# Loading the second quarter of w by row set instead of by quadrant, in a matmul with a decayed running sum

## The chip, the cores and the metric

One core of one Trainium2 chip runs the whole problem. The metric is the device time of one launch in microseconds (us). The engines are named as in the profile: PE (TensorE), with PEld for its weight loads, DVE (VectorE), ACT (ScalarE), POOL (GpSimd) and SP (SyncE). PE, DVE, ACT and POOL compute; SP, ACT and POOL also issue transfers (DMAs), which 16 DMA engines carry out.

## The reference

```python
B, S, D = 16, 2048, 1024          # x: (B, S, D), w: (D, D), decay: (D,), all float32
xw = x @ w
out[:, 0, :] = xw[:, 0, :]
for t in range(1, S):
    out[:, t, :] = decay * out[:, t - 1, :] + xw[:, t, :]
```

## The kernel before, in words

The kernel works on x in 64 chunks of 512 time steps, two chunks to a group. POOL loads a chunk as bfloat16 (`load`, L105), DVE transposes it in 32 by 32 blocks (`turn`, L115), ACT or DVE regroups it into the tile `xt` (`part`, L123), and PE multiplies it with w (`matmul`, L131). For each of the eight blocks n of 128 output columns PE sums eight contraction blocks k into PSUM. DVE then scans along time with the decays, ACT and POOL help with half of the positions, DVE transposes back and SP stores. The work of each engine is written out by hand: a dictionary `agenda` (L520) names, for each step, a string of deeds that is performed in that order, and every instruction is pinned to its place.

The change lies in the first deeds, `agenda[-99]` (L521), which begin

```python
-99: "M0 M1 U0 M2 M3 U1 U2 w0 W1 w2 W3 K0 K1 K2 K3 E0 E1 G0 ... G7 q4 w5 Q4 W6 W7 D E8 ..."
```

`M` is `load_half`: half a chunk of x in four transfers of 128 KB, one per quadrant (32 partitions). M0 and M1 are the halves of chunk 0, M2 and M3 those of chunk 1. `U` is `load_part`: one quarter of w. All of these are issued by POOL, in this order, on one queue. The program gives POOL's transfers eight semaphores in turn, so each of them waits, before it is issued, until the POOL transfer eight places ahead has landed: U0 waits for M0, M2 for M1, M3 for U0, U1 for M2, U2 for M3.

w is stored as bfloat16 in `wsb`. A quarter (h, e) of it is the column half h (512 columns) of the rows of parity e. The quarter (0, 0) is loaded by SP and ACT at the very start; U0, U1 and U2 are the quarters (0, 1), (1, 0) and (1, 1). In the staging tile, partition 32q + p holds, for m = 0 to 3, the row 256q + 64m + 2p + e of w. The 128 rows of one m, 32 out of each of the four 256-row bands q, are called a row set here. They are exactly the contraction block k = 2m + e, and are copied into `wsb` by one deed per m (`settle`, L326): `W` on DVE, `w` on ACT. For U0 the deeds are `q4` and `Q4` (the row set m = 0, split at L375 into the columns of n = 0 and the rest), `w5`, `W6` and `W7` (m = 1, 2, 3). For U1 they are W8 to W11 on DVE, for U2 they are w12 to w15 on ACT.

PE begins with dummy matmuls (`spin`, L344). Then, for n = 0 to 3, it takes the even k of chunk 0 (both halves, L633), then the odd k of chunk 0 (L636), which are the ones that need U0, then all k of the first half of chunk 1 (L640, which needs the deeds E8 to E11, the transposes of M2), then the second half (L644, which needs E12 to E15, the transposes of M3). After these it goes on to n = 4 and above, even k first (which need W8 to W11), then odd k (which need w12 to w15).

The functions that the diff touches, with the line numbers of the profile:

Of the kernel before, what the change touches and what calls it, by code (L numbers as in the profile page):

```python
# [14 lines left out]
def _ap(ap_obj: bass.AP, new_ap, extra_offset=0):  # L15
    return dataclasses.replace(
        ap_obj,
        ap=[list(p) for p in new_ap],
        offset=ap_obj.offset + extra_offset,
    )  # L20
# [5 lines left out]
def kernel(  # L26
# [26 lines left out]
    nc = tc.nc  # L53
    pin = tc.keep_in_program_order
    B, S, D = x.shape
    assert w.shape == (D, D)

    NQ = 4
    P = 32
    CQ = D // NQ  # L60
    K = CQ // P
    M = K // 2
# [4 lines left out]
    CH = D // 2  # L67
# [12 lines left out]
    def quad(q):  # L80
        return slice(q * P, (q + 1) * P)
# [59 lines left out]
    class Tile:  # L141
# [39 lines left out]
        def copy(self):  # L181
            self.xs = sb.tile([128, 2 * TL], FP32, name=f"xs{self.lot % 3}")[:, 0:self.T]
            parts = self.ps if isinstance(self.ps, tuple) else (self.ps,)
            size = self.T // len(parts)
            for i, ps in enumerate(parts):
                pin(nc.scalar.copy(out=self.xs[:, i * size:(i + 1) * size], in_=ps))  # L186
# [99 lines left out]
    class Outlet:  # L286
# [8 lines left out]
        def store(self, b, t0):  # L295
# [4 lines left out]
            for j in range(0, self.nj, nj):  # L300
# [11 lines left out]
    stage = {(0, 0): room[0][:, 0:size],  # L312
             (0, 1): room[0][:, size:size * 3 // 2].bitcast(BF16),
             (1, 0): room[1][:, 0:size // 2].bitcast(BF16),
             (1, 1): room[1][:, size // 2:size].bitcast(BF16)}

    def load_w(queues, h, e):
        for i, q in enumerate((0, 2, 1, 3)):
            pin(queues[i % len(queues)].dma_start(  # L319
                out=stage[h, e][quad(q)].rearrange("p (m d) -> p m d", m=M),  # L320
                in_=_ap(w, [[2 * D, P], [2 * P * D, M], [1, CH]],
                        (q * CQ + e) * D + h * CH)))

    def settle(h, e, m, copy):
        src = stage[h, e][:, m * CH:(m + 1) * CH]
        pin(copy(out=wcols[:, 2 * m + e, h],  # L326
                 in_=src.rearrange("p (q r i) -> p q r i", q=NQ, r=R)))
# [21 lines left out]
    for q in range(NQ):  # L349
        pin(nc.sync.dma_start(  # L350
            out=rows[q * P:q * P + R],
            in_=_ap(decay, [[P, R], [CH, 2], [1, P]], q * CR)))
# [8 lines left out]
        spin(3 if q < NQ - 1 else 2, gates[q])  # L361

    def load_part(i):
        load_w((nc.gpsimd,), *((0, 1), (1, 0), (1, 1))[i])

    def part_one(i, copy):
        part(i // 8, copy, i % 4, i % 4 + 1, *halves[i // 4 % 2])
# [1 line left out]
    def settle_one(i, copy):  # L369
        settle(i // 8, i // 4 % 2, i % 4, copy)  # L370
# [102 lines left out]
    def turn_and_load(c):  # L473
# [16 lines left out]
        "w": lambda i: settle_one(i, nc.scalar.copy),  # L490
        "M": load_half,
        "U": load_part,
        "E": lambda i: turn(i // 8, *halves[i // 4 % 2], i % 4, i % 4 + 1),
        "F": lambda i: part_one(i, nc.vector.tensor_copy),
# [229 lines left out]
```

## Time and profile before

| | |
|---|---|
| median of 3 runs | 903.8 us (903.74 to 904.62) |
| the profiled execution | 903.77 us, span 902.0 us |
| granted TensorE clock | 1.0 |
| PE busy | 892.4 us (99%) |
| DVE, ACT, POOL busy | 824.9 (91%), 687.6 (76%), 656.6 (73%) us |
| POOL's transfers of w (L319, U0 to U2) | 12 of 128 KB, median 5.1 us from issue to landing |
| POOL's half-chunk transfers of x (M0 to M3) | 16 of 128 KB, median 5.9 us |

The span runs from the first to the last instruction that the profiler saw. Idle time of an engine other than the one that sets the end costs nothing by itself. In the lines of the time view, the first column is the start in us from the span's start, the second the duration, and the bracket at the end tells how long the engine had been idle before, and what ended that.

### The profile page before, as it was taken

Reading aid. Unit: us, or ns where it says so; the run is one execution under the profiler, and the core shown is the slowest. Engines: PE = TensorE matmul, PEld = TensorE weight load, DVE = VectorE, ACT = ScalarE, POOL = GpSimd, SP = SyncE. Lnnn points to the kernel's source line nnn. Section 1 sums busy time; section 2 is a strip of 40 time slices with the busy share of each in tenths; the row PEclk is TensorE's granted clock in tenths of the full one; section 3 lists DMA queues with packets and bytes.
Section 4 is the critical chain, followed back from the end, with each engine's and each line's share of the span. In section 5 each row is a group of like instructions: output and inputs, shape, how many; then the busy total and the mean of one; then the engine's idle time right before and its main releaser. Section 6 shows DMA issues by size and latency. Waiting matters only on the chain.

```text
span 902.0 us, 12224 instructions
## 1 busy us (share of the span) xinstructions
PE 892.4 (99%) x4127; PEld 412.1 (46%) x4209; DVE 824.9 (91%) x635; ACT 687.6 (76%) x962; POOL 656.6 (73%) x755
## 2 busy tenths in 40 slices
PE   9999999999999999999999999999999999999998
PEld 5544444444444444444444444444444444444444
DVE  4999998999999999999998999999999999999998
ACT  4889967777877877878778778777787787787743
POOL 7888678777767778777677686777777777776532
PEclk9999999999999999999999999999999999999999
DMA  9999999999999999999999999999999999999858
GB/s 191 194 215 220 229 243 218 215 218 249 244 243 254 231 258 251 251 243 250 225 234 227 223 234 224 232 228 226 233 230 227 227 231 225 226 228 222 176 146 239
DMA packets 403182, 204.77 MB, mean 227 GB/s; under 512 B 9392, under 2 KB 402096, under 8 KB 403120
## 3 DMA queue, kind: packets, MB, share of 16 engines
q1 hardware_dynamic: 265808, 134.77, 60.6%
q0 software_dynamic: 137024, 68.70, 56.9%
q8 instruction: 33, 0.54, 0.2%
q10 hardware_dynamic: 288, 0.52, 0.2%
q14 instruction: 29, 0.24, 0.1%
HBM read 138.42 MB, written 134.22 MB: 302 GB/s over the span
## 4 chain that ended last, share of the span: by engine, by line
PE 97%; DMA 1%; issue 1%; POOL 0%; DVE 0%; ACT 0%; DVEq 0%; POOLq 0%
PE ps L131 96%; PE spare L131 1%; DMA xb<-in_x_dram 1%; DMA ot<-in_w_dram 1%; POOL ot L319 0%; DVE so L233 0%; POOL xb L105 0%; PE ps L415 0%; PE spare L415 0%; ACT xb L422 0%; DVE wsb L375 0%; DVEq L375 0%; POOLq L708 0%
## 5 line engine op out<-in xcount | busy, mean ns | idle before, releaser
L131 PE MATMUL ps<-xt,wsb 128*128 128x512 bf16 x3934 | 860.8, 378 | 4.5 <-DVE wsb L375 0.2
L131 PEld LDWEIGHTS <-wsb 128*128 128x128 bf16 x4160 | 406.7, 98 | 478.7 <-ACT wsb L326 0.8
L208 POOL TENSOR_TENSOR xs<-h,xs 128x512 f32<-128x512 f32 (+1 forms) x190 | 242.8, 1278 | 188.2 <-ACT h L169 85.0
L186 ACT COPY xs<-ps 128x1024 f32<-128x1024 f32 (+1 forms) x190 | 188.8, 994 | 153.6 <-PE ps L131 143.2
L278 DVE STREAM_TRANSPOSE ot<-so 128x1024 f32<-128x1024 f32 (+2 forms) x264 | 300.2, 1175 | 2.3 <-POOL so L202 1.1
L266 POOL TENSOR_TENSOR so<-h,xs 128x512 f32<-128x512 f32 (+1 forms) x190 | 241.1, 1271 | 42.6 <-ACT h L169 27.1
L123 ACT COPY xt<-xw 128x2048 bf16<-128x2048 bf16 (+1 forms) x136 | 242.3, 1790 | 7.8 <-DVE xw L115 7.8
L105 POOL DMA_DIRECT2D xb<-in_x_dram x264 | 173.9, 660 | 3.4 <-DMA ot<-in_w_dram 1.3
L169 ACT ACTIVATE h<-so,dec 128x512 f32<-128x512 f32 (+1 forms) x190 | 145.5, 766 | 27.8 <-DVE so L213 24.5
L115 DVE STREAM_TRANSPOSE xw<-xb 128x2048 f32<-128x2048 f32 (+1 forms) x78 | 147.3, 1901 | 6.7 <-DMA xb<-in_x_dram 6.7
L213 DVE TENSOR_TENSOR_SCAN so<-spare,keep,xs 128x512 f32<-128x512 f32 (+1 forms) x97 | 119.9, 1239 | 26.7 <-POOL xs L208 26.3
L213 DVE TENSOR_TENSOR_SCAN so<-spare,xs 128x512 f32<-128x512 f32 x93 | 113.3, 1220 | 27.2 <-POOL xs L208 24.4
L169 ACT ACTIVATE h<-ps,dec 128x512 f32<-128x512 f32 (+1 forms) x189 | 129.5, 685 | 0.0
L233 DVE TENSOR_TENSOR_SCAN so<-dec,ps 128x1024 f32<-128x1024 f32 x34 | 76.9, 2260 | 0.8 <-ACT h L169 0.6
L233 DVE TENSOR_TENSOR_SCAN so<-dec,keep,ps 128x1024 f32<-128x1024 f32 (+2 forms) x35 | 74.7, 2137 | 0.0
L270 ACT COPY keep<-so 128x1 f32<-128x1 f32 x136 | 25.2, 188 | 9.2 <-DVE so L233 8.7
L204 ACT COPY so<-keep 128x1 f32<-128x1 f32 x97 | 18.4, 191 | 2.5 <-DVE ot L278 2.3
L131 PE MATMUL spare<-xt,wsb 128*128 128x512 bf16 (+1 forms) x64 | 12.9, 332 | 0.0
L131 PE MATMUL ps<-xw,wsb 128*128 128x256 bf16 (+1 forms) x68 | 11.2, 301 | 0.0
L202 POOL MEMSET so<- 128x1 f32 x93 | 10.7, 117 | 0.6 <-DVE ot L278 0.6
L319 POOL DMA_DIRECT2D ot<-in_w_dram x12 | 6.5, 545 | 3.6 <-DMA xb<-in_x_dram 2.5
L344 PE MATMUL spare<-idle 128*128 128x512 bf16 x22 | 7.1, 499 | 1.2 <-DVE idle L334 1.2
(40 smaller groups left out, 40.5 us busy)
## 6 DMA issues: line engine op xcount, KB each, us to landing
out_dram<-ot SPq DMA_DIRECT2D x236, 512.0 KB, 11.1
xb<-in_x_dram POOLq DMA_DIRECT2D x248, 256.0 KB, 7.9
out_dram<-ot SPq DMA_DIRECT2D x56, 128.0 KB, 2.6
xb<-in_x_dram POOLq DMA_DIRECT2D x16, 128.0 KB, 5.9
out_dram<-ot SPq DMA_DIRECT2D x8, 256.0 KB, 4.5
ot<-in_w_dram POOLq DMA_DIRECT2D x12, 128.0 KB, 5.1
out_dram<-xb SPq DMA_DIRECT2D x4, 256.0 KB
ot<-in_w_dram ACTq DMA_DIRECT2D x2, 256.0 KB, 5.2
```

Source lines behind the costliest of these rows:

```text
L105: pin(nc.gpsimd.dma_start(out=xb_of[c][quad(q), j0:j1], in_=_ap(x, [[D, P], [P * D, j1 - j0], [1, CQ]], (b * S + t0 + j0 * P) * D + q * CQ)))
L115: pin(nc.vector.transpose(out=dst.rearrange("p (m j i) -> p j m i", m=M, i=P)[:, j0:j1, m0:m1], in_=src.rearrange("p (j m c) -> p j m c", ...
L123: pin(copy(out=xt_of[c][:, m0:m1, :, j0 * P:j1 * P], in_=src))
L131: pin(nc.tensor.matmul(out=ps[:, t0:t1] if ps.shape[1] >= t1 else ps, lhsT=lhs, rhs=rhs, start=(k == 0 and t0 == start), stop=(k == K - 1),))
L169: pin(nc.scalar.activation(out=h, in_=src, func=mybir.ActivationFunctionType.Copy, scale=dec[:, self.n:self.n + 1]))
L186: pin(nc.scalar.copy(out=self.xs[:, i * size:(i + 1) * size], in_=ps))
L208: pin(nc.gpsimd.tensor_tensor(out=odds, in0=self.g, in1=odds, op=ALU.add))
L213: pin(nc.vector.tensor_tensor_scan(out=so[:, 3:T + 2:2], data0=squares[-1][:, n:n + 1].to_broadcast([128, T // 2]), data1=self.xs[:, 1:T:2 ...
L233: pin(nc.vector.tensor_tensor_scan(out=so[:, t + 2:t + 2 + size], data0=dec[:, n:n + 1].to_broadcast([128, size]), data1=ps, initial=befor ...
L266: pin(nc.gpsimd.tensor_tensor(out=self.so[:, 2:T + 2:2], in0=self.h, in1=self.xs[:, 0:T:2], op=ALU.add))
L270: pin(nc.scalar.copy(out=self.keep, in_=self.so[:, self.T + 1:self.T + 2]))
L278: pin(nc.vector.transpose(out=outlet.ot[:, :, c0:c0 + P], in_=self.so[:, 2 + t0:2 + t0 + nj * P].rearrange("p (i t) -> p i t", t=P)))
```

## The change

Before, each of the three quarters that POOL loads is fetched by `load_w`, in four transfers, one per quadrant q: 32 partitions, and in each of them the four rows m. After, the quarter U0 is fetched by a new function `load_rows`, in four transfers, one per row set m: all 128 partitions, one row of 512 elements in each. The other two quarters are fetched as before. Each transfer still moves 128 rows of 512 float32 elements and stores them as bfloat16, so 128 packets of 1024 bytes and 128 KB.

```diff
     def load_w(queues, h, e):
         for i, q in enumerate((0, 2, 1, 3)):
             pin(queues[i % len(queues)].dma_start(
                 out=stage[h, e][quad(q)].rearrange("p (m d) -> p m d", m=M),
                 in_=_ap(w, [[2 * D, P], [2 * P * D, M], [1, CH]],
                         (q * CQ + e) * D + h * CH)))
 
+    def load_rows(h, e):
+        for m in range(M):
+            pin(nc.gpsimd.dma_start(
+                out=stage[h, e][:, m * CH:(m + 1) * CH],
+                in_=_ap(w, [[CQ * D, NQ], [2 * D, P], [1, CH]],
+                        (2 * m * P + e) * D + h * CH)))
+
...
     def load_part(i):
-        load_w((nc.gpsimd,), *((0, 1), (1, 0), (1, 1))[i])
+        if i == 0:
+            load_rows(0, 1)
+        else:
+            load_w((nc.gpsimd,), 1, i - 1)
```

The number and the order of the instructions on every engine stay as they were. What changes are the semaphores that the settling instructions wait for: before, q4 on DVE and w5 on ACT each waited for all four transfers of U0 (and Q4, W6 and W7 stood behind q4); after, q4 waits for the first transfer alone, w5 for the second, W6 for the third, W7 for the fourth. The issuing waits on POOL are the same as before by position: M3's four issues still wait for the four transfers of U0, one each.

In the access patterns, the outermost count of the transfer is 32 on both sides before. After, it is 128 on the side of the staging tile and 4 on the side of w, whose 128 rows lie in four bands and can't be told as one regular step.

## Prediction

> **What bounds the kernel now.** I read the page's busy shares and its chain first. PE is busy for 892.4 of 902.0 us, and the chain that ended last is PE's own matmuls:
>
> ```profile
> PE 892.4 (99%) x4127; PEld 412.1 (46%) x4209; DVE 824.9 (91%) x635; ACT 687.6 (76%) x962; POOL 656.6 (73%) x755
> ...
> PE 97%; DMA 1%; issue 1%; POOL 0%; DVE 0%; ACT 0%; DVEq 0%; POOLq 0%
> ```
>
> Then PE's waits from 2 us to the end. The view lists two, and one of them is for the quarter of w that the change touches (L375 is q4):
>
> ```profile
> PE spare L344 <- ACT gate L360: 0.3, 1, 0.3
> PE ps L131 <- DVE wsb L375: 0.2, 1, 0.2
> ```
>
> So a change to the loading can take from the time only what PE idles in the first 30 us. Whatever makes PE late there, on the other hand, is carried to the end, because PE has no slack later. Next I read the time view around the wait:
>
> ```profile
> 14.69 0.27 PE L131 MATMUL spare<-xw,wsb 128*128 128x256 bf16 x1
> 14.86 0.62 ACT L326 COPY wsb<-ot 128x512 bf16<-128x512 bf16 x1 [0.23 <-DMA ot<-in_w_dram]
> 14.88 0.36 DVE L375 COPY wsb<-ot 128x128 bf16<-128x128 bf16 x2 [0.66 <-DMA ot<-in_w_dram]
> 15.13 2.27 PEld L131 LDWEIGHTS <-wsb 128*128 128x128 bf16 x12 [0.45 <-DVE wsb L375]
> 15.13 0.82 PE L131 MATMUL ps<-xt,wsb 128*128 128x512 bf16 x2 [0.17 <-DVE wsb L375]
> ```
>
> The last even-k matmul starts at 14.69. Its neighbours start 0.113 apart, so the next could start at 14.81; it starts at 15.13. PE loses **0.33 us** here. The cause is the landing of U0: its four transfers are issued at 8.21, 9.12, 9.65 and 10.18 and take 4.6, 4.3, 4.4 and 4.6 us, so they land at 12.8, 13.4, 14.0 and 14.8, and q4 starts 0.1 after the last one. DVE had been free since 14.23 and ACT since 14.63.
>
> Last, the same view where the last quarter of w (U2) is needed:
>
> ```profile
> 26.54 2.17 ACT L326 COPY wsb<-ot 128x512 bf16<-128x512 bf16 x4
> ...
> 28.76 0.33 PEld L131 LDWEIGHTS <-wsb 128*128 128x128 bf16 x3 [0.35 <-ACT wsb L326]
> ```
>
> U2's last transfer is issued at 20.47 and takes 5.9 us: it lands at 26.4. The four copies w12 to w15 start at 26.54, and PE's odd k of n = 4 follow right behind them: the matmul at 28.76 comes 0.240 and the one after it 0.227 after the one before, where the regular step is 0.216. PE is already late by 0.035 us at this place.
>
> **The change part by part.**
>
> *The issues on POOL.* Four issues go, at 0.54 us each (L319), and four come. They hold 128 packets each as before, so I take 0.54. The bounds are SP's issue of a w transfer (0.38) and the longest of POOL's x issues (0.73): -0.6 to +0.8 us over the four. This is hidden. M2 is issued from 10.82 on, and its first transfer lands at 15.4 (4.6 later), behind everything ahead of it: the DMA share is 9 tenths or more in every slice from 11 to 40 us, and landings follow each other by 0.55 to 0.72 us whatever the issue times are. If that backlog were gone, the 0.8 us would reach E8, which has 0.54 us of slack (its transpose ends at 18.06, its first matmul starts at 18.60): 0.3 us at worst.
>
> *The waits.* If the transfers still spread over the DMA engines as the old ones do, the row sets land at 12.8, 13.4, 14.0 and 14.8. q4 starts when DVE has finished F6, at 14.23 instead of 14.88, and takes 0.2, so the odd k start when PE has finished the even ones, at 14.81. w5 starts at 14.63 and ends at 15.25; its matmuls are due at 14.81 + 4 x 0.216 = 15.67. Q4 and W6 follow q4 on DVE and end by 14.9; k = 5 is due at 16.5. W7 starts at 14.9, after the landing at 14.8, and ends at 15.2; k = 7 is due at 17.4. Nothing new is late here: PE gains 0.33.
>
> *What is late next.* PE, 0.33 ahead, asks for E8 at 18.27 (ready 18.06), for E12 at 21.83 (20.76), for W8 at 25.39 (24.54): all there. Then it asks for w12 at 25.39 + 8 x 0.216 = 27.12. w12 can't move up by 0.33, because its data lands at 26.4: with the 0.1 us that the other copies take from landing to start (14.76 to 14.86) it starts at 26.49 instead of 26.54. w12 to w15 take 2.17 us together, w15 ends 0.05 earlier than now, and PE's k = 7 can start 0.05 earlier. **Of 0.33 us, 0.05 stay.** The landing of U2 doesn't move, since the same number of packets lies ahead of it.
>
> *The packets.* Their number and size are the same. Row sets write 128 partitions at a time instead of 32, and no transfer of this shape is in the trace. If it were faster, U2 would land earlier and the whole 0.33 + 0.035 = 0.36 us would stay: that is the ceiling of any gain. If it were slower, E8 is the first to feel it, from 0.54 us on.
>
> The sum is -0.05 us on the profiled execution's 903.77, which is 0.03 under the median: **903.7 us**.
>
> *A row that speaks against this.* How a transfer is divided among the 16 DMA engines may hang on its outermost count, and that falls to 4 on the side of w. The profile has one kind of transfer with an outermost count of 4, the decays on SP's queue (8 packets each). ACT's queue, over the whole run, and SP's, from 0 to 8 us, show:
>
> ```profile
> q10 hardware_dynamic: 288, 0.52, 0.2%
> ```
> ```profile
> q1 hardware_dynamic: 336, 0.53, 24.7%
> ```
>
> 288 is two w transfers of 128 rows and 16 completion packets each. 336 is 256 + 32 of data and 48 more: 32 for the two w transfers, which leaves 4 for each of the four decay transfers. So a transfer with an outermost count of 4 closed on four DMA engines. Those are on another queue, and have 4 on both sides; the rows of POOL's queue can't tell. [...]
>
> **The rivals.**
>
> *B: each row set is carried by four DMA engines, each by another four.* The load of the 16 stays even. A quadrant transfer brings 8 packets to each engine and the landings are 0.64 us apart on average (12.8 to 14.8), so 80 ns a packet. A row set then brings 32 packets to each of its four engines: 2.56 us from 12.2 on, when the x ahead of it is through, so all four land near 14.8. q4 and w5 start as now and nothing is gained. M3 is issued on U0's landings: its first issue moves from 13.28 to 14.8 and its last from 15.05 to 16.5. The shortest x half takes 4.6 us from issue to landing, so M3's last lands at 21.1 at the latest (now 20.2): from 0, if its place behind M2 (17.5) hides it, to 0.9 us. E12 has slack for that, but all that is queued behind it, U2 and w12 too, would be as much later, and w12 has none: 0 to +0.9 us, of which I take 0.3, since most of the 4.6 is queueing: 904.1. For it: the decays. Against: the staging tile's side of the transfer has 128 partitions.
>
> *C, the slower one: all four row sets on the same four DMA engines.* These get 128 packets of U0 instead of 32: 10.2 us, from 12.2 to 22.4. M2, behind it on them, takes four times 0.66 more and lands at 25.0 instead of 17.5. E8 ends at 25.6, and PE goes on there at 25.6 instead of 18.6: **+7.0 us, 910.8**. Later deeds have slack by then (M3 lands at 27.7, PE needs E12 at 29.2). It decides as soon as any engine is more than E8's 0.54 us behind. For it: the decays' packets don't say which four. Against: nothing in the trace piles up like that.
>
> *D: the rest.* Quicker packets (up to -0.36: 903.4), dearer issues (+0.3: 904.1), or something that I don't see.
>
> **How the numbers follow.** The forecast gets 0.42, B 0.30, C 0.18, D 0.10. A measurement of this kernel can tell about 0.2% (1.8 us) from no change. The forecast, 0.29 of B and 0.07 of D lie within that: 0.78. Slower: C, 0.01 of B and 0.01 of D: 0.20. Faster by over 1.8 us would need idle time of PE that the profile doesn't have: 0.02. The range goes from 903.2 (the ceiling of the gain, with 0.2 for the difference between runs) to 905.6 (B's 0.9 on the median, and the 0.9 between the lowest and the highest of the three runs). It leaves out C and the faster 0.02.
>
> **What would show it.** Forecast: q4 starts near 14.23 and PE's first odd k at 14.81; PEld waits longer for w12 to w15, and PE's matmuls after 29 us stand within 0.1 us of where they stand now. B: q4 still starts near 14.9, the four landings of U0 lie within some 0.3 us, and M3 is issued over 1 us later. C: the landings of U0 spread over 10 us, to 22, and DVE waits for x up to 25. Wrong would be all of it if PE's waits after 30 us changed, or if the packets of U0 took another time than 80 ns per engine.

## The result, and the profile after

| | before | after |
|---|---|---|
| median | 903.77 us (8 runs, 903.53 to 904.62) | 905.85 us (8 runs, 905.15 to 908.07) |
| ratio | | 1.0026, 95% interval 1.0015 to 1.0037 |
| profiled execution, its span | 903.77, 902.0 us | 905.71, 903.9 us |
| packets on POOL's queue over the run | 137024 | 138560 |
| M0's last transfer lands | 9.80 | 9.28 |
| M1's last transfer lands | 12.37 | 12.23 |
| U0's four transfers land | 12.84, 13.39, 14.04, 14.76 | 14.13, 14.39, 15.71, 17.20 |
| M2's last transfer lands | 17.49 | 19.92 |
| U2's last transfer lands | 26.37 | 27.83 |

The change costs 2.1 us. The forecast of no measurable difference was wrong, and the time lies 0.25 us above the range. The two traces tell most of it.

PE's waits from 2 us to the end, after the change. The columns are the engine, line and tile that waited, what ended the wait, the total in us, how often, and the longest:

```profile
PE ps L131 <- DVE xw L115: 1.9, 1, 1.9
PE ps L131 <- DVE wsb L333: 0.2, 1, 0.2
```

The wait for q4 is gone (L375 has become L385). In its place stand a small wait for W7, and one of 1.9 us for a transpose of x, E8. The time views of DVE and of PE from 14 us on show the order in which this happens; each bracket tells how long the engine was idle and for what. First E8 on DVE and the first matmul on chunk 1 before the change:

```profile
17.62 1.42 DVE L115 STREAM_TRANSPOSE xw<-xb 128x256 f32<-128x256 f32 x4 [1.35 <-DMA xb<-in_x_dram]
18.60 0.84 PE L131 MATMUL ps<-xw,wsb 128*128 128x256 bf16 x6
```

Then DVE and PE after it:

```profile
14.16 0.36 DVE L385 COPY wsb<-ot 128x128 bf16<-128x128 bf16 x2
15.73 0.29 DVE L333 COPY wsb<-ot 128x512 bf16<-128x512 bf16 x1 [1.21 <-DMA ot<-in_w_dram]
17.23 0.29 DVE L333 COPY wsb<-ot 128x512 bf16<-128x512 bf16 x1 [1.20 <-DMA ot<-in_w_dram]
...
20.04 1.43 DVE L115 STREAM_TRANSPOSE xw<-xb 128x256 f32<-128x256 f32 x4 [1.96 <-DMA xb<-in_x_dram]
```
```profile
14.56 0.27 PE L131 MATMUL spare<-xw,wsb 128*128 128x256 bf16 x1
14.67 0.81 PE L131 MATMUL ps<-xt,wsb 128*128 128x512 bf16 x2
...
17.58 0.82 PE L131 MATMUL ps<-xt,wsb 128*128 128x512 bf16 x3 [0.16 <-DVE wsb L333]
18.23 0.38 PE L131 MATMUL spare<-xt,wsb 128*128 128x512 bf16 x1
20.54 0.84 PE L131 MATMUL ps<-xw,wsb 128*128 128x256 bf16 x6 [1.93 <-DVE xw L115]
```

q4 starts at 14.16 and PE goes from the even to the odd k (14.56, 14.67) without a gap: the 0.33 us of before are gained. Then the row sets m = 2 and m = 3 come late: W7 starts at 17.23, and k = 7 starts 0.32 us late. The large loss follows behind them: E8 starts at 20.04 instead of 17.62, because M2 lands 2.43 us later, and PE's first matmul on chunk 1 starts at 20.54 instead of 18.60. That is +1.94, and the span is 1.9 longer. Nothing behind it adds to that or gives it back. In the profile after, x happens to come 0.52 us earlier (M0's last landing at 9.28 instead of 9.80), so that counted from there M2 is 2.95 us later.

So U0 holds up the queue, with the same 512 pieces of data. The issues on POOL take longer (below), but they are not the reason: M2's last transfer is issued at 12.52, and at 12.72 before. The totals of POOL's queue over the whole run (packets, MB, share of the 16 engines), before and after:

```profile
q0 software_dynamic: 137024, 68.70, 56.9%
```
```profile
q0 software_dynamic: 138560, 68.71, 56.7%
```

There are 1536 packets more, and with them not even 0.01 MB. The DMA view from 10.5 to 17.5 us shows where they are, before and after:

```profile
DMA packets 2316, 1.36 MB, mean 195 GB/s; under 512 B 166, under 2 KB 2316, under 8 KB 2316
```
```profile
DMA packets 3164, 1.04 MB, mean 149 GB/s; under 512 B 1658, under 2 KB 3164, under 8 KB 3164
```

In these 7 us 1492 more packets are smaller than 512 bytes (in the trace they have 4 bytes, and a record of 9 ns each), and 0.32 MB less is moved. The traces do not tell which DMA engine carries a packet, so what is said of single engines, here and in the experiments, is an estimate from the counts. 1536 is 4 transfers x 12 DMA engines x 32: it is as if four engines carry the 128 rows of a row set, 32 each, and each of the other twelve gets one empty packet for every row that one of the four carries. Over the 16 engines that is 96 for each. From 10.5 to 12.75 us there are 813 packets under 512 bytes (53 before the change), from 12.75 to 15.75 us 809 (70 before). So 760 empty ones are early and 739 late, half and half. If an engine works through its queue in order, which is assumed here and was not shown, it takes those of the sets ahead of its own data early and the others after it. If the four sets have four engines each to themselves, 4 x (0 + 32 + 64 + 96) = 768 are early. If all four sets had the same four engines (rival C), all 1536 would be.

### The profile page after: what moved, and what is told of

Read it like the earlier page. It is cut to its first block, busy times and chain, and to the rows that moved or that the text cites. A ratio compares the mean times of both kernels' runs of the same rounds, so it can differ in the third digit from the quotient of the medians.

```text
span 903.9 us, 12220 instructions
## 1 busy us (share of the span) xinstructions
PE 892.7 (99%) x4127; PEld 412.3 (46%) x4209; DVE 825.7 (91%) x635; ACT 687.1 (76%) x962; POOL 657.0 (73%) x755
## 3 DMA queue, kind: packets, MB, share of 16 engines
q0 software_dynamic: 138560, 68.71, 56.7%
## 4 chain that ended last, share of the span: by engine, by line
PE 97%; DMA 1%; issue 1%; POOL 0%; DVE 0%; ACT 0%; DVEq 0%; POOLq 0%
PE ps L131 95%; DMA xb<-in_x_dram 1%; PE spare L131 1%; POOL ot L326 0%; POOL xb L105 0%; DVE so L233 0%; PE ps L425 0%; DVE xw L115 0%; PE spare L425 0%; ACT xb L432 0%; DVEq L115 0%; POOLq L718 0%
## 5 line engine op out<-in xcount | busy, mean ns | idle before, releaser
L115 DVE STREAM_TRANSPOSE xw<-xb 128x2048 f32<-128x2048 f32 (+1 forms) x78 | 147.4, 1901 | 6.5 <-DMA xb<-in_x_dram 6.5
```

The source lines that it names most:

```text
L115: pin(nc.vector.transpose(out=dst.rearrange("p (m j i) -> p j m i", m=M, i=P)[:, j0:j1, m0:m1], in_=src.rearrange("p (j m c) -> p j m c", ...
```

## The experiments

Three theories stood after that. **Theory 1**: the split over four engines with its empty packets is what holds up the queue, and it comes from the outermost count of 4 on the side of w. **Theory 2**: writing 128 partitions at a time, or the waits by row set, is what hurts. **Theory 3**: the sharing is uneven, some engines carry two row sets, and the empty packets cost nothing.

**32 bands instead of 4.** One line of `load_rows` is changed, here and in the next two runs, with 8 and 2 in the place of 32:

```diff
-                in_=_ap(w, [[CQ * D, NQ], [2 * D, P], [1, CH]],
-                        (2 * m * P + e) * D + h * CH)))
+                in_=_ap(w, [[D // 32 * D, 32], [2 * D, 128 // 32], [1, CH]],
+                        (256 // 32 * m + e) * D + h * CH)))
```

> Row sets as in the change (one transfer per settling step, all 128 partitions at once), but with the 128 rows taken from 32 bands of w instead of 4, so that the outermost count on the side of w is 32. All rows of the quarter are loaded once, to other partitions: the kernel computes with a w whose rows in this quarter are permuted. Theory 1 (empty packets): a transfer with outermost count 4 is carried by four DMA engines, and the other twelve get one 4-byte packet for each of its 32 rows per engine; these 96 packets per engine hold up the x behind them by about 2.4 us. With 32 bands there are none: the software queue has 137024 packets again, M2 lands near 17.5, time 903.7 (903.4 to 904.0). Theory 2 (128 partitions at a time, or the waits by row set, slow the load): nothing changes here, 905.8 and M2 at 19.9. Theory 3 (uneven sharing: some DMA engines carry two row sets, others none, and the empty packets cost nothing): 903.7 as theory 1.

Measured: 903.36 us, ratio 0.9995 (0.9986 to 1.0004); 137024 packets; row sets at 12.72, 13.33, 13.96 and 14.68; M2's last at 17.40. DVE's time view from 13.85 us on:

```profile
13.85 0.43 DVE L385 COPY wsb<-ot 128x128 bf16<-128x128 bf16 x2
14.21 0.27 DVE L333 COPY wsb<-ot 128x512 bf16<-128x512 bf16 x1
14.71 0.29 DVE L333 COPY wsb<-ot 128x512 bf16<-128x512 bf16 x1 [0.23 <-DMA ot<-in_w_dram]
...
17.52 0.77 DVE L115 STREAM_TRANSPOSE xw<-xb 128x256 f32<-128x256 f32 x2 [1.96 <-DMA xb<-in_x_dram]
```

This is the forecast's picture, to 0.1 us in each landing: q4 right after F6, W6 without a wait, E8 where it was before the change. So 128 partitions at a time and waits by row set do not bring the delay, and theory 2 falls. What the outermost count does is not settled by this run alone between theories 1 and 3. The gain of 0.5 us is not distinguished from none.

**8 bands.**

> The same with 8 bands (outermost count 8), again with the rows of this quarter permuted. Theory 1: eight engines carry a row set with 16 rows each, the other eight get 16 empty packets: 128 per transfer, 512 in all (software queue 137536 packets), 32 per engine. At 25 ns each M2 is 0.8 us late (18.3), less E8's slack of 0.54: time 904.1 (903.8 to 904.4). Theory 2: 905.8. Theory 3: 903.8 if the eights are shared evenly, 904.5 if three of the four row sets meet on one half of the engines (48 packets instead of 32, 1.3 us late).

Measured: 904.14 us, ratio 1.0004 (0.9995 to 1.0013); 137536 packets, as said; M2's last at 18.20. Theory 1 has the count, the landing and the time. The time alone would not decide, as its interval holds both no change and theory 3's values. The order of the packets says more about theory 3. From 10.75 to 11.75, on to 13.4 and on to 14.5 us there are 154, 288 and 156 packets under 512 bytes (25, 40 and 25 before the change), so 129, 248 and 131 empty ones. If the two halves of the engines carry two row sets each, in turn, 128, 256 and 128 are expected, by the same reckoning as above; with three sets on one half no order of the sets gives this. So the uneven sharing of theory 3 is not seen.

**2 bands.**

> The same with 2 bands (outermost count 2), rows of this quarter permuted. Theory 1: two engines carry a row set with 64 rows each, the other fourteen get 64 empty packets: 896 per transfer, 3584 in all (software queue 140608). The slowest engines have 64 data packets (2.6 us more than 32) and 192 empty ones (4.8 us): M2 7.4 us late, time 910.6 (909 to 912). Theory 2: 905.8. Theory 3: 64 data packets on eight engines, 2.6 us late, 905.8; if two row sets meet on the same two engines, 128 packets, 910.9.

Measured: 908.14 us, ratio 1.0053 (1.0038 to 1.0069); 140608 packets, as said; M2's last at 21.48. The count fits theory 1, the time does not: it is 2.5 us less than expected. Theory 2 (905.8) and theory 3 (905.8 or 910.9) miss it too. Of the empty packets some 2780 come from 10.5 to 15 us and 740 from 15 to 18 us; if each set has another pair of engines, 2816 and 768 are expected. From M1's last landing to M2's it takes 9.2 us here and 5.1 us before the change. If an engine has 64 data packets of a row set instead of 32, at the 80 ns a packet that the landings before the change give, 2.6 of the 4.1 us more are theirs. That leaves, as an estimate, 1.5 us for 192 empty packets, 8 ns each, not 25. So the price in theory 1 was wrong, which says nothing yet against its cause: 25 ns was all of the change's delay divided by 96, and something else had to be in that delay.

**Quadrants from 4 bands.** This takes the empty packets to the old shape. The price was now put as three theories, 1a to 1c:

```diff
-        for m in range(M):
+        for q in (0, 2, 1, 3):
             pin(nc.gpsimd.dma_start(
-                out=stage[h, e][:, m * CH:(m + 1) * CH],
-                in_=_ap(w, [[CQ * D, NQ], [2 * D, P], [1, CH]],
-                        (2 * m * P + e) * D + h * CH)))
+                out=stage[h, e][quad(q)].rearrange("p (m d) -> p m d", m=M),
+                in_=_ap(w, [[60 * D, 4], [2 * D, P], [1, CH]],
+                        (q * CQ + e) * D + h * CH)))
```

> The quarter by quadrant again, as before the change (32 partitions, four rows each), but with the 128 rows taken from 4 bands 60 rows apart, so that the outermost count on the side of w is 4 and the staging tile is written as before. Some rows of w are loaded twice and others not at all, so this quarter of w is another one. The 1536 empty packets should be there as with the change. Theory 1a (the empty packets alone cost the time, some 25 ns each): M2 lands near 19.9 and the time is 905.8. Theory 1b (an empty packet costs only the 9 ns that its record shows, 0.9 us for 96; the other 1.5 us come from the four row sets writing the same partitions in the same order at the same time, which quadrants do not): M2 near 18.3, time 904.2. Theory 1c (the other 1.5 us come from reading rows of w that lie a power of two apart): 904.2 too, as these bands do not.

Measured: 905.90 us, ratio 1.0022 (1.0012 to 1.0032); 138560 packets; U0 lands at 14.67, 14.96, 15.28 and 16.11, M2's last at 19.17. The 1536 empty packets are there although the transfer writes a quadrant, so in these runs they go with the 4 on the side of w (137024 packets with 32 there, with quadrants and with row sets alike). M2 lies between 1a and 1b. The time is not evidence for 1a, because PE loses it at another place here:

```profile
PE ps L131 <- DVE wsb L385: 1.4, 1, 1.4
PE spare L351 <- ACT gate L367: 0.4, 1, 0.4
PE ps L131 <- DVE xw L115: 0.2, 1, 0.2
PE ps L131 <- DVE wsb L333: 0.2, 1, 0.2
```

With quadrants, q4 waits for all four transfers again, and the last lands at 16.11 instead of 14.76.

**Bands 250 rows apart**, one number changed (`250 * D` for `CQ * D`):

> The change with its four bands 250 rows apart instead of 256 (some rows of w loaded twice, others not at all). Everything else as in the change. Theories 1a and 1b: nothing changes, 905.8 and M2 near 19.9. Theory 1c: the 1.5 us go, 904.2 and M2 near 18.3.

Measured: 906.41 us, ratio 1.0027 (1.0016 to 1.0038); M2's last at 20.30. As with the change: 1c falls.

**Row sets that are one regular step.** A version that loads by row set and computes what the reference asks for:

```diff
# turn: the transpose's input
-            in_=src.rearrange("p (j m c) -> p j m c", m=M, c=P)[:, :, m0:m1]))
+            in_=src.rearrange("p (j c m) -> p j m c", m=M, c=P)[:, :, m0:m1]))
# load_w
-                in_=_ap(w, [[2 * D, P], [2 * P * D, M], [1, CH]],
+                in_=_ap(w, [[2 * M * D, P], [2 * D, M], [1, CH]],
# load_rows
-                in_=_ap(w, [[CQ * D, NQ], [2 * D, P], [1, CH]],
-                        (2 * m * P + e) * D + h * CH)))
+                in_=_ap(w, [[2 * M * D, 128], [1, CH]],
+                        (2 * m + e) * D + h * CH)))
```

> Row sets whose 128 rows are one regular step: the contraction rows are given to partitions in another way, for x and w alike (partition p, set m and parity e hold row 8p + 2m + e), so that each of the four transfers has 128 as its outermost count on both sides. The transposes of x take their input with a step of 4 elements instead of 1. Theory 1 in all its forms: no empty packets (137024 on the software queue), row sets land near 12.8, 13.4, 14.0, 14.7, no wait of PE for them: 903.4 (903.0 to 903.9), as with 32 bands. If the strided input makes the transposes slower than 1901 ns (DVE is 91% busy), the time is longer: 78 of them.

Measured: 931.68 us, ratio 1.0305 (1.0291 to 1.0319). The loading does what was expected (137024 packets, row sets 0.65 us apart, no wait of PE for w), but the transposes with a strided input cost far more than that is worth. The costliest groups, before the change and here (busy us in all, mean ns of one):

```profile
L115 DVE STREAM_TRANSPOSE xw<-xb 128x2048 f32<-128x2048 f32 (+1 forms) x78 | 147.3, 1901 | 6.7 <-DMA xb<-in_x_dram 6.7
```
```profile
L115 DVE STREAM_TRANSPOSE xw<-xb 128x2048 f32<-128x2048 f32 (+1 forms) x78 | 259.8, 3343 | 3.0 <-DMA xb<-in_x_dram 3.0
```

112 us more of work on DVE, which was 91% busy, is 27.5 us more of time.

**The row sets alone at the head of the queue.**

```diff
-    load_w((nc.sync, nc.scalar), 0, 0)
...
         if i == 0:
             load_rows(0, 1)
+            load_w((nc.gpsimd,), 0, 0)
...
-        -99: "M0 M1 U0 M2 M3 U1 U2 ..."
+        -99: "U0 M0 M1 M2 M3 U1 U2 ..."
```

> A probe of the four row-set transfers alone: they are the first thing on the software queue, with the quarter (0, 0) moved behind them on the same queue, so nothing else runs beside them (the start of the kernel is later by some microseconds, its time is not the question). If each row set has four DMA engines of its own, data packets of 1024 bytes run on 4, then 8, 12 and 16 engines (12, 24, 36 and 48 packets per 250 ns) as the issues come, each set for 2.7 us. If two row sets share engines, there are never more than 12 engines' worth, and the last set ends 2.7 us after the first of the same engines. Theory 1a: sets 1 to 3 begin up to 0.8, 1.6 and 2.4 us after their issue arrives, as their engines have 32, 64 and 96 empty packets first; theory 1b: 0.3, 0.6 and 0.9.

Measured: the sets land at 6.69, 8.61, 10.72 and 11.31, and the data packets never pass 27 per 250 ns. That is neither the 48 of separate engines nor a clear 36 with one set ending 2.7 us after another. Some data packets last 0.5 to 1.9 us instead of the usual 0.1, although nothing else is on the queue ahead of them. The probe doesn't decide what it was made for. It shows that the row sets' data packets are held up even without x beside them.

**The price of empty packets by themselves.** Two kernels without the change, with four further transfers of small pieces behind U0 that nobody uses:

```diff
     def load_part(i):
         load_w((nc.gpsimd,), *((0, 1), (1, 0), (1, 1))[i])
+        for m in range(M if i == 0 else 0):
+            scrap = const.tile([128, 32, 4], BF16, name=f"scrap{m}")
+            pin(nc.gpsimd.dma_start(              # second kernel: 16 and 8 for 4 and 32
+                out=scrap[0:4, 0:32],
+                in_=_ap(w, [[32 * D, 4], [D, 32], [1, 4]], m * 128 * D)))
```

> The kernel before the change, with four further transfers on POOL between U0 and M2 that nobody uses: 128 pieces of 8 bytes each, with outermost count 4. By theory 1 they bring each DMA engine 32 small data packets and 96 empty ones, and no two of them compete for anything large. To be read against e10_crumbs16, which has the same 128 pieces per transfer with outermost count 16, so 32 small data packets per engine and no empty ones. The difference in M2's last landing is the price of 96 empty packets by themselves: theory 1a (25 ns each) 2.4 us, theory 1b (9 ns each) 0.9 us; 16 ns, 1.5 us, is what the quadrant run with four bands would suggest. Software queue: 1536 packets more than e10_crumbs16.

> The partner of e9_crumbs4 without empty packets: 512 small data packets more than before the change and 64 completion packets (137600 on the software queue). M2 lands later than before by the small packets and the four further issues alone; all theories agree here.

Measured: 139136 and 137600 packets, so the 1536 again. M2, which was to be read, is not clean: in these kernels its issues wait for U0, and without empty packets it lands at 15.90, 16.62, 18.03 and 18.87, with a hole in the middle. The further transfers themselves can be read. Their issues and times to landing, with the empty packets and without:

```profile
L367 POOL DMA_DIRECT2D scrap<-in_w_dram x4: 682/690/712, 10.5 to 12.6; - x4
DMA to landing us min/median/max: 5.0/5.6/5.9
```
```profile
L367 POOL DMA_DIRECT2D scrap<-in_w_dram x4: 524/526/529, 10.3 to 12.2; - x4
DMA to landing us min/median/max: 3.0/3.7/4.4
```

From the last landing of U0 to theirs it takes 2.27 us (15.26 to 17.53) with the empty packets and 0.72 us (14.56 to 15.28) without: 1.55 us for the 1536 empty packets, which at 96 for each engine is 16 ns each. But U0's own last landing, just ahead of them on the queue, is late as well: it comes 3.04 us after M1's (12.22) with the empty packets and 2.59 us after M1's (11.97) without. Counted from M1's last landing, the difference is 2.0 us, 21 ns each. So **96 empty packets for each engine cost 1.55 to 2.0 us here, 16 to 21 ns each**, by one profile of each kernel. The theory that they cost nothing, theory 3, falls with this. The two kernels also write the small pieces to 4 and to 16 partitions; the small packets themselves last 25 ns in both.

**All three quarters by row set** (`load_part` calls `load_rows` for each):

> U1 and U2 by row set as well, so three quarters instead of one. If each quarter by row set delays what is behind it on the queue by the 2.4 us of the change, U2 lands 7 us late, and the copies w12 to w15, which have no slack, carry this to PE: 903.9 + 7 = 911 (909 to 912). Rival: only U0 hurts, because M2 is due right behind it and everything later has slack: 905.8 to 906.5. Software queue 141632 packets (4608 empty ones).

Measured: 909.84 us, ratio 1.0067 (1.0050 to 1.0084), beside 903.48 for the kernel before: +6.4; 141632 packets, as said. U2's last lands at 32.41 (26.37 before the change). PE's waits show that E8 and the copies w12 to w15 both count now:

```profile
PE ps L131 <- DVE xw L115: 2.8, 2, 1.6
PE ps L131 <- ACT wsb L333: 1.7, 2, 1.5
PE ps L131 <- ACT xt L123: 0.8, 1, 0.8
```

The first line holds two waits: 1.2 us at 13.73 for a transpose of M1's data, which stands ahead of U0 on the queue, and 1.6 us at 20.79 for E8. U2 is 6.0 us late and not 7: at M3's last landing (22.94 instead of 20.19) it is 2.75, so U1 and U2 add 3.3 together. So the delay belongs to each quarter loaded in this way, and the rival that only U0 hurts falls.

**Two further profiles**, of the quadrants from 4 bands and of the change, for the spread between profiles:

> A second look at quadrants from 4 bands, for the spread between profiles. So far M2's last landing comes 6.7 us after M1's here, 7.7, 7.4 and 7.1 with row sets from 4 bands, and 5.0 to 5.3 without empty packets. If the 96 empty packets cost 1.5 us everywhere and row sets add something of their own, this is 6.4 to 6.9 again. If quadrants and row sets cost the same, it lies between 7.0 and 7.7.

> A second look at the change itself, beside e12_quad4_look on the same chip: 7.0 to 7.7 us from M1's last landing to M2's, by either theory.

Measured: 6.92 us for the quadrants, at the edge of either range, and 7.13 us for the change. The profiles together, in us:

| profile | empty packets per DMA engine that has data (estimate) | M1's last to U0's last landing | M1's last to M2's last landing | M0's last to M2's last landing |
|---|---|---|---|---|
| no empty packets (before; 32 bands; regular step) | 0 | 2.39, 2.60, 2.25 | 5.12, 5.32, 4.97 | 7.69, 8.03, 7.72 |
| row sets, 8 bands | 32 | 3.20 | 5.73 | 8.57 |
| quadrants, 4 bands (two profiles) | 96 | 3.67, 3.56 | 6.73, 6.92 | 9.76, 10.02 |
| row sets, 4 bands (change, 250 rows, all rows, second profile of the change) | 96 | 4.97, 5.05, 4.34, 4.42 | 7.69, 7.41, 7.06, 7.13 | 10.64, 10.89, 10.71, 10.30 |
| row sets, 2 bands (64 data packets for 32) | 192 | 6.51 | 9.25 | 12.15 |

Against the mean of the first row (2.41, 5.14 and 7.81), the quadrants with empty packets hold up M2 by 1.7 us, which is near the 1.55 that 96 empty packets cost by themselves. The row sets hold it up by 2.2 us, so 0.5 us more, and U0's own last landing by 2.3 instead of 1.2. M1's last landing is itself late wherever U0 has empty packets (2.85 to 3.65 us after M0's, instead of 2.57 to 2.75), so the count from M1 leaves a part out. From M0's, which lands before the first empty packet, the quadrants hold up M2 by 2.1 us, the row sets by 2.8, so 0.7 us more; the 2.1 are near the 2.0 of the small pieces. That rest of 0.5 to 0.7 us is not explained. It is there with bands 250 rows apart too. In three of the four row-set profiles from 4 bands single data packets last 1.5 to 2.0 us, where the quadrants' longest took 0.9; in the fourth, the second profile of the change, none of U0's lasts over 0.5, and U0's last landing is within 0.1 us of that with all quarters by row set. That the four sets get in each other's way by writing the same partitions in the same order was only argued, and these packets do not bear it out.

## Why the prediction was wrong

- **"The packets. Their number and size are the same."** This is the step that failed, in the forecast and in rival B alike. The data packets are the same 512, but 1536 empty ones come with them, 96 for each DMA engine if they are spread evenly. They cost 1.6 to 2.1 us of the queue's time, and row sets a further 0.5 to 0.7 us, for which no cause is shown. The prediction counted what the kernel asks for, not what the queue makes of it.
- **Which engines carry a row set.** The forecast took all 16 as the likeliest. The row that spoke against it, the decays' four completion packets, pointed the right way. With 128 partitions on the side of the tile and 2, 4, 8 and 32 bands on the side of w, 896, 384, 128 and 0 packets were added per transfer, and 384 with the quadrants from 4 bands too. That is 7, 3, 1 and 0 for each of the 128 rows, and it fits splits over 2, 4, 8 and 16 engines by the reckoning above. This is an estimate from these counts; the engines themselves are not in the traces.
- **Rival B** named the split that the counts fit, another four engines for each set (760 empty packets early, 739 late), but priced it as if a row set's 32 packets per engine began at once: "all four land near 14.8". They landed at 14.1, 14.4, 15.7 and 17.2. If the last set's engines had 96 empty packets ahead of its data, at 16 to 21 ns each, that is 1.5 to 2.0 us more, so 16.3 to 16.8; the rest up to 17.2 is not explained. B's price of 0 to 0.9 us was put on M3's late issue. M3 was issued later, as B said (14.42 to 17.49 instead of 13.28 to 15.05), but that cost nothing: it still landed 2.7 us behind M2, as before.
- **Rival C** had a split that the counts do not fit (all sets on the same four engines, M2 7.5 us late) and the right path: "It decides as soon as any engine is more than E8's 0.54 us behind". M2 came 2.43 us later, less 0.54 us of slack gives 1.89, and PE's first matmul on chunk 1 moved by 1.94.
- **The waits.** Right: q4 follows F6 (14.16), PE's first odd k follows the last even one, and 0.33 us are gained there. With the change this was lost again at k = 7 (0.32 us), which the prediction had due at 17.4 with W7 at 14.9; W7 came at 17.23.
- **"Of 0.33 us, 0.05 stay"** could be seen with 32 bands only, where nothing else is in the way. There the time is 0.5 us less than before, with an interval from -1.3 to +0.4 us, so neither 0.05 nor the ceiling of 0.36 is shown. U2 landed at 25.64 in that profile, and PE had no listed wait at all.
- **The issues on POOL.** Taken as 0.54 each, they are 0.68 (L326, 668 to 711 ns), inside the bounds, and hidden as said. The spacing of landings given there, 0.55 to 0.72 us, does not hold everywhere behind M2: before the change U1's last transfer lands 2.04 us after its third (22.08, 24.12).

## What to carry to other kernels

Before a transfer is reshaped, look at the outermost count of its access pattern on both sides, and measure what the new one brings: here 128 partitions on the side of the tile did not help when the side of w began with 4 (1536 more packets and 2.1 us; with 32 bands no more packets and no measurable loss). The packet count of the queue told at once that the transfers carried more than their data (138560 for 137024), where the MB were the same (68.71 for 68.70). And the cost of a transfer need not fall on those who wait for it: here the waits for the reshaped transfers got shorter at first (q4 at 14.16 instead of 14.88), and the time was lost on the next transfer in the queue (M2, 2.43 us later).

## What the runs showed of the hardware that was not expected

- The four row-set transfers of U0 brought 512, 1536 and 3584 more packets on POOL's queue with 8, 4 and 2 bands on the side of w, and none with 32; with 4 they have 4 bytes each. With 4 they cost 16 to 21 ns each where they were measured by themselves (at 96 for each engine, the estimate above), and their record shows 9. With 2 the same estimate leaves some 8 ns for each, so these runs do not give one price, and why is open.
- M1's transfers, which stand just ahead of U0 on the queue, landed late too: the last of them came 2.57 to 2.75 us after M0's without empty packets and 2.85 to 3.65 us with them. PE waited for M1's data with all quarters by row set (1.2 us), in the second profile of the change (0.6), with bands 250 rows apart (0.4) and with the quadrants (0.2 in one of two profiles), but not in the first profile of the change. How this comes about is open.
- The issue of a row set on POOL took longer with more empty packets: 0.55 us with none (32 bands), 0.61 with 128, 0.68 with 384 and 0.81 with 896 empty packets per transfer. A quadrant with 384 took 0.79 to 0.83, so the number of empty packets alone does not set it.
- The 32 by 32 block transposes on DVE (L115) took 1.76 times as long with a step of four elements in their input (3343 ns for 1901 ns on average, over the same shapes).
